# Layer B's value product: the low pass with 72 weight columns, issued between transposes, two half steps behind a head's last transposes

## The chip, the cores and the metric

One core of one Trainium2 chip runs the kernel. The metric is the device time of one execution in microseconds (us); smaller is better. Runs of one kernel differ by about 0.2%.

## What is computed

Two attention layers of a streaming encoder, over a prompt of 2048 tokens and a sample of 64 tokens, with model width 1024. Each layer normalises x, makes queries, keys, values and a gate by one input projection, attends, multiplies by the gate, projects out and adds x. The change touches layer B (the second one): 16 heads of 64 dimensions, each 64-token chunk attends to itself and the 8 chunks before it. For one chunk of one head, cut to what matters:

```python
s = einsum('bqkgd,bskd->bkgqs', q, k) * 64**-0.5 + bias   # scores
p = softmax(where(valid, s, NEG_INF))
o = einsum('bkgqs,bskd->bqkgd', p, v)                      # value product
y = x + (o * silu(gate)) @ w_out
```

## The kernel before

All matrix products are done on TensorE (PE) with 32-bit numbers split in two parts, a high part that the fast format holds and a low part, the rest. A product of two such numbers is then high x high, high x low and low x high.

**Units and heads.** Layer B works on `its`, 72 items: 8 pairs of heads, each over 9 units (eight units of 256 prompt tokens, as two tiles of 128, and the sample of 64 tokens, which comes ahead of the last prompt unit). Within an item the loop of `pipeline` (L1199) runs over four steps `y`: tile 0 and tile 1 of the first head, then of the second; the sample has two steps.

**What a step does.** `scores` (L1080) multiplies queries by keys into a bank `sb` of PSUM; DVE adds the bias and takes the row minimum (L1114), ACT takes the exponential (L1118). Then comes filler: the projections of later units, cut in small pieces (`filler.to`, lines L481 to L483), paced by `goal`. Then `values` (L1135) for the step before: one transpose of p on PE per 128 keys (up to five, all recorded at the helper's line L597), and `split_to`: ACT writes the high part `ph` (L569), DVE the low part `pl` (L570). `ph` and `pl` have two buffers each, one per head.

**The value product.** `outputs` (L1163) takes one head of one unit, all its tiles together. V lies in `VT` with 128 columns per 128 keys: 64 of its high part, 64 of its low part. For each block of keys it issues two products with the same 128 weight columns, one that streams `ph` (L1188) and one that streams `pl` (L1189), so all four combinations are summed. A full unit has four blocks that stream 256 columns and two that stream 128. The first head's product opens the bank `o` (one buffer). With the second head, `outputs` first transposes the gate `G` into the bank `tp` (L1171 to L1173; ACT reads it in `gate_t`, L973), and after the product `finish_pairs` runs: two copies on ACT (L981), two additions on DVE (L983), one product on POOL (L984), one store on SP's queue (L985).

**Where the product stands.** A head whose last transposes were issued in one step has its product in the step after (`nxt`, `pend`): the first head's at y = 3, the second head's at y = 1 of the next unit.

**The bank tp.** It has one buffer, and `queries` (L1042) uses it too, at the end of step y = QY = 1 (for the sample y = 0), for the next unit: four transposes, then four ACT operations on the bank (L1062, L1063), and `low`, as background work, for each of two heads: two DVE operations that read the bank (L1067, L1071) and one that doesn't (L1075).

**What sets the order.** On PE the order of the program is kept (`manual_schedule`); on the other engines a planner orders the instructions by data and by a simulated timeline. Background work (`bg`) waits in a list; `bg.share` issues some of it after each `scores` and `values`, and it is tied behind the step's last work on that engine.

Of the kernel before, what the change touches and what calls it, by code (L numbers as in the profile page):

```python
# [15 lines left out]
P = 128  # L16
# [10 lines left out]
HD = 64  # L27
# [12 lines left out]
AL, AP_ = 0.7, 4  # L40
BL, BP_ = 1.8, 4
FR = 0.6
KEEP = [1, 1] + [0] * (NU - 1)

PACE_B = 2.45
# [6 lines left out]
def hybrid_encoder_kernel(  # L52
# [32 lines left out]
    nc = tc.nc  # L85
# [14 lines left out]
    def psum(tag, cols, bufs, pool=None):  # L100
        uid[0] += 1
        return (pool or pp).tile([P, cols], F32, tag=tag, name=f"{tag}_{uid[0]}", bufs=bufs)
# [174 lines left out]
    bg = Background()  # L277
# [317 lines left out]
    def transpose(out, in_):  # L595
        n = in_.shape[0]
        nc.tensor.transpose(out, in_, ident[:n, :n])  # L597
# [390 lines left out]
    def layer_b():  # L988
# [53 lines left out]
        def queries(it):  # L1042
            for q in it.todo:
                bg.run(q)
            u, T, tiles = it.unit
            gk = ksc[:, 1:2]
            if u == 1:
                load_cache(ckt_b[it.hp], cv_b[it.hp], CB, True)
            tp = psum("tp", 512, 1)
            for pr, (tt, t0, n) in zip(it.prs, tiles):  # L1050
                for j in range(2):
                    transpose(tp[:, j * T + t0 : j * T + t0 + n], pr[:n, j * P : (j + 1) * P])
            it.q1 = q1 = t("q1", [P, 2, UT], 2, F32R)
            it.q2 = q2 = low_queries().rearrange("p (h s) -> p h s", h=2)
            if u == NU:
                kd = [a[:, CB : CB + TS] for a in (KSA, KSB)]
            else:
                kd = [a[:, u * UT : (u + 1) * UT] for a in (KA, KB)]
            qt = [tp[r, 0:T] for r in halves]
            kt = [tp[r, T : 2 * T] for r in halves]  # L1060
            for hh, rows in enumerate(halves):
                nc.scalar.activation(q1[rows, hh, :T], qt[hh], AF.Identity, scale=qsc[rows, 1:2])  # L1062
                nc.scalar.activation(kd[hh][rows], kt[hh], AF.Identity, scale=gk[rows])  # L1063

            def low(hh, rows):
                def fn():
                    nc.vector.scalar_tensor_tensor(  # L1067
                        q2[rows, hh, :T], qt[hh], qsc[rows, 1:2], q1[rows, hh, :T].bitcast(F32),
                        op0=ALU.mult, op1=ALU.subtract,
                    )  # L1070
                    nc.vector.scalar_tensor_tensor(  # L1071
                        kd[hh][halves[1 - hh]], kt[hh], gk[rows], kd[hh][rows].bitcast(F32),
                        op0=ALU.mult, op1=ALU.subtract,
                    )
                    nc.vector.tensor_copy(q1[halves[1 - hh], hh, :T], q1[rows, hh, :T].bitcast(F32))  # L1075
                return fn

            it.todo = [bg.put(1.0, low(hh, rows), True) for hh, rows in enumerate(halves)]

        def scores(it, i, h):  # L1080
            u, T, tiles = it.unit
# [50 lines left out]
                        op=ALU.mult,  # L1132
                    )

        def values(it, i, h):  # L1135
            u, T, tiles = it.unit
            last = u == NU
            tt, t0, n = tiles[i]
            if i == 0:
                it.ph[h] = t("ph", [P, 6, 256], 2, F32R)  # L1140
                it.pl[h] = t("pl", [P, 6, 256], 2, F32R)
            if last:
                sizes, kb = [P, P, TS], 0
            else:
                kt0 = max(tt - 4, 0)
                sizes, kb = [P] * (tt - kt0 + 1), kt0 - it.base
            PT = psum_b("sb", 1024, 2)
            PTv = PT.rearrange("p (c x) -> p c x", x=P)
            for c, kn in enumerate(sizes):
                transpose(PTv[:kn, c, :n], it.p[i, h][:n, c * P : c * P + kn])  # L1150
            full = sum(kn == P for kn in sizes)
            groups = [(0, full, P)]
            if last:
                groups.append((2, 1, TS))
            for c, m, kn in groups:
                bg.anchor(*split_to(
                    it.ph[h][:kn, kb + c : kb + c + m, t0 : t0 + n],
                    it.pl[h][:kn, kb + c : kb + c + m, t0 : t0 + n],
                    PTv[:kn, c : c + m, :n],
                ))  # L1160
            it.sizes = sizes

        def outputs(it, h):  # L1163
            u, T, tiles = it.unit
            last = u == NU
            n = tiles[0][2]
            sizes = it.sizes
            if h == 0:
                it.O = psum("o", 512, 1)
            else:  # L1170
                GT = psum("tp", 512, 1)  # L1171
                for e, (_, t0, _) in enumerate(tiles):
                    transpose(GT[:, t0 : t0 + n], it.G[:n, e * P : (e + 1) * P])  # L1173
                gt = gate_t(GT[:, :T].rearrange("p (j s) -> p j s", j=1), T)
            mm = []
            if last:
                for c, kn in enumerate(sizes):
                    mm.append((VS[:kn, c, h], c, kn, 0, TS))
            else:
                ta, tb = tiles[0][0], tiles[1][0]  # L1180
                for kt in range(max(tb - 4, 0), ta + 1):
                    mm.append((VT[:, kt, h], kt - it.base, P, 0, UT))
                if ta >= 4:
                    mm.append((VT[:, ta - 4, h], ta - 4 - it.base, P, 0, P))
                mm.append((VT[:, tb, h], tb - it.base, P, P, UT))
            for x, (vt, c, kn, q0, q1_) in enumerate(mm):
                dst = it.O[:, h * T + q0 : h * T + q1_]
                nc.tensor.matmul(dst, vt, it.ph[h][:kn, c, q0:q1_], start=x == 0, stop=False)  # L1188
                nc.tensor.matmul(dst, vt, it.pl[h][:kn, c, q0:q1_], start=False, stop=x == len(mm) - 1)  # L1189
            if h == 1:  # L1190
                finish_pairs(
                    it.O[:, : 2 * T].rearrange("p (j e s) -> p j e s", j=1, e=2),
                    gt,
                    T,
                    og[1][:, it.hp : it.hp + 1, u * UT : u * UT + T],
                )
                finished[1, u] = finished.get((1, u), 0) + 1

        def pipeline():  # L1199
            filler.attending = False  # L1200
            bg.lazy = True
            for q in Q2:
                zero(q[0:64, 256:512])
            filler.to(its[1].mark - 5.12)
            queries(its[0])
            filler.to(its[1].mark)
            filler.attending = True
            prev = pend = None
            for x, it in enumerate(its):
                heads = [(i, h) for h in range(2) for i in range(len(it.unit[2]))]  # L1210
                c0 = filler.done
                end, near = c0 + (PACE_B if len(heads) == 4 else PACE_S) * len(heads), 1e9
                if x + 2 < len(its):
                    near = its[x + 2].mark
                    if len(its[x + 1].unit[2]) + len(its[x + 2].unit[2]) < 4:
                        near += MORE
                    end = max(its[x + 2].mark, min(end, its[x + 3].mark - 1.0 if x + 3 < len(its) else end))

                def goal(s):
                    filler.to(c0 + min((end - c0) * s / (2 * len(heads)), (near - c0) * s / NS))  # L1220

                for y, (i, h) in enumerate(heads):
                    scores(it, i, h)
                    bg.share(BL, BP_)
                    goal(2 * y + 1)
                    nxt = None
                    if prev is not None:
                        values(*prev)
                        bg.share(BL, BP_)
                        if prev[1] == len(prev[0].unit[2]) - 1:  # L1230
                            nxt = prev[0], prev[2]
                    prev = it, i, h
                    if pend is not None:
                        outputs(*pend)
                    pend = nxt
                    goal(2 * y + 2)
                    if y == (QY if len(heads) == 4 else QS) and x + 1 < len(its):
                        queries(its[x + 1])
                        near = 1e9
                assert x + 2 >= len(its) or its[x + 2].ready  # L1240
            values(*prev)
            filler.to(filler.done + 2.6)
            if pend is not None:
                outputs(*pend)
            filler.to(filler.done + 2.6)
            outputs(prev[0], prev[2])

        return pipeline

# [175 lines left out]
```

## Time and profile before

| | |
|---|---|
| time, median of 3 runs | 2327.18 us (2323.96 to 2329.47) |
| profiled execution, span | 2323.8 us |
| what lies around the span | 3.4 us, median less span |
| instructions | 42433 |
| TensorE granted clock, mean | 0.998 |
| layer B's attention | from about 905 to 2166 us (first and last L1188) |

The profile is one execution on the chip. PE is a matmul, PEld the load of its weights; a load runs beside the matmul before it. The time of a matmul in a row is a modelled one and overlaps the next one's; what it costs in a stream is read from the distance between starts. In a group's row stand the line, the engine, the operation, what it writes and reads, the shape and the count, then busy time, the mean of one in ns, and after the second bar the idle time of the engine before it and what ended that. In a timeline's row stand start, duration (us), engine and line; idle time stands in brackets. In a row by windows the last three figures are the granted clock of TensorE, the DMA engines' share and GB/s.

### The profile page before, as it was taken

The page shows a single profiled execution, that of the slowest core. Times are in us where ns is not written, and L with a number is a line of the kernel's source. Part 1 is how long each engine was busy: PE and PEld are TensorE (multiplying, and loading weights), DVE is VectorE, ACT ScalarE, POOL GpSimd, SP SyncE. Part 2 cuts the span into 40 slices and gives each one's busy share as a digit, 9 for nine tenths or more (in the row PEclk, how much of TensorE's full clock was granted, in tenths as well). Part 3 has the DMA queues.
Part 4 walks back from the last instruction along what each step waited for, and adds up shares of the span by engine and source line. Part 5 has one row for each costly group of instructions (what it writes and reads, how often), then busy time and mean ns, then how long its engine had stood idle before and what let it go on. Part 6 is the DMA issues. An engine that isn't in the chain of part 4 may idle for free.

```text
span 2323.8 us, 42433 instructions
## 1 busy us (share of the span) xinstructions
PE 2269.6 (98%) x13981; PEld 1985.2 (85%) x13981; DVE 1547.3 (67%) x5214; ACT 1432.7 (62%) x3644; POOL 847.6 (36%) x1194
## 2 busy tenths in 40 slices
PE   8899999999999998999999999999999999999999
PEld 7787888888889997878888888888888888888999
DVE  7679988887782228876766767767667677676211
ACT  7778777777772236765665656656656566566321
POOL 5554533333254446432222222222222222224443
PEclk9999999999999999999999999999999999999999
DMA  8846446754446776453444533534435435433664
GB/s 256 263 146 207 162 144 195 229 167 162 134 126 204 226 216 219 145 186 126 158 142 128 161 127 114 178 126 152 143 123 163 134 103 177 131 126 106 189 186 148
DMA packets 232126, 379.37 MB, mean 163 GB/s; under 512 B 24721, under 2 KB 163361, under 8 KB 231873
## 3 DMA queue, kind: packets, MB, share of 16 engines
q1 hardware_dynamic: 231904, 376.65, 51.3%
q8 instruction: 110, 1.80, 0.3%
q14 instruction: 112, 0.91, 0.1%
HBM read 296.13 MB, written 82.08 MB: 163 GB/s over the span
## 4 chain that ended last, share of the span: by engine, by line
PE 77%; DVE 10%; ACT 5%; DMA 5%; issue 2%; POOL 1%; SPq 0%; POOLq 0%; ACTq 0%; DVEq 0%
PE pj L481 13%; PE pj L483 12%; PE pj L482 12%; PE pj L1283 5%; PE pj L1284 5%; PE pj L1285 5%; PE sb L597 5%; PE o L1189 3%; PE o L1188 3%; PE tp L597 3%; PE sb L1110 3%; PE sb L1111 3%; PE sa L597 2%; DVE sq L524 1%; DVE p L1114 1%
## 5 line engine op out<-in xcount | busy, mean ns | idle before, releaser
L481 PE MATMUL pj<-wh,xx 128*128 128x512 f32 (+1 forms) x1648 | 668.7, 406 | 15.2 <-DVE ms L433 7.2
L483 PE MATMUL pj<-wh,xx 128*128 128x512 f32 (+1 forms) x1648 | 638.1, 387 | 0.0
L482 PE MATMUL pj<-wl,xx 128*128 128x512 f32 (+1 forms) x1648 | 635.0, 385 | 0.0
L483 PEld LDWEIGHTS pj<-wh,xx 128*128 128x128 f32 x1648 | 310.4, 188 | 67.3
L481 PEld LDWEIGHTS pj<-wh,xx 128*128 128x128 f32 x1648 | 311.9, 189 | 56.9 <-ACT pb L504 6.5
L386 POOL TENSOR_TENSOR xx<-xraw,xx 128x528 fp32r<-128x528 f32 (+1 forms) x200 | 265.6, 1344 | 218.2 <-ACT xx L385 212.0
L482 PEld LDWEIGHTS pj<-wl,xx 128*128 128x128 f32 x1648 | 312.5, 190 | 37.7
L528 POOL TENSOR_TENSOR f<-f,mhalf 128x4 f32<-128x4 f32 (+3 forms) x221 | 227.9, 1031 | 228.7 <-DVE f L524 216.9
L1118 ACT ACTIVATE p<-p,nm 128x640 f32<-128x640 f32 (+5 forms) x272 | 204.4, 751 | 167.2 <-DVE nm L1114 165.1
L1283 PE MATMUL pj<-xx,wh 128*128 128x264 f32 x1024 | 293.3, 286 | 0.1
L1284 PE MATMUL pj<-xx,wh 128*128 128x264 f32 x1024 | 291.3, 284 | 0.0
L1285 PE MATMUL pj<-xx,wl 128*128 128x264 f32 x1024 | 289.8, 283 | 0.0
L1114 DVE CUSTOM_DVE_ANT_0 p<-sb,BT 128x640 f32<-128x640 f32 (+5 forms) x272 | 196.7, 723 | 119.6 <-PE sb L1111 116.2
L570 DVE TENSOR_TENSOR pl<-sb,ph 128x640 fp32r<-128x640 f32 (+5 forms) x288 | 196.8, 683 | 116.1 <-ACT ph L569 113.7
L385 ACT CAST xx<-xraw 128x528 fp32r<-128x528 f32 (+1 forms) x200 | 123.4, 626 | 220.3 <-PE pj L1285 131.9
L984 POOL TENSOR_TENSOR o<-gt,o 128x256 f32<-128x256 f32 (+2 forms) x140 | 107.4, 767 | 371.3 <-issue 149.0
L569 ACT CAST ph<-sb 128x640 fp32r<-128x640 f32 (+5 forms) x288 | 167.1, 580 | 122.4 <-PE sb L597 114.0
L1288 DVE TENSOR_TENSOR res<-pj,res 128x264 f32<-128x264 f32 x128 | 55.1, 431 | 246.5 <-PE pj L1285 230.7
L1283 PEld LDWEIGHTS pj<-xx,wh 128*128 128x128 f32 x1024 | 192.7, 188 | 0.8 <-DVE res L1288 0.3
L1285 PEld LDWEIGHTS pj<-xx,wl 128*128 128x128 f32 x1024 | 192.6, 188 | 0.0
L1284 PEld LDWEIGHTS pj<-xx,wh 128*128 128x128 f32 x1024 | 192.4, 188 | 0.2
L524 DVE CUSTOM_DVE_ANT_0 sq<-pa 128x64 f32<-128x64 f32 (+1 forms) x850 | 170.2, 253 | 22.1 <-ACT pa L504 20.0
(189 smaller groups left out, 4810.5 us busy)
## 6 DMA issues: line engine op xcount, KB each, us to landing
xx<-xsb SPq DMA_DIRECT2D x224, 512.0 KB, 4.1
xx<-xsa SPq DMA_DIRECT2D x88, 512.0 KB, 4.8
xraw<-oga SPq DMA_DIRECT2D x64, 264.0 KB, 3.4
xraw<-ogb SPq DMA_DIRECT2D x64, 264.0 KB, 3.3
xsa<-xx SPq DMA_DIRECT2D x32, 512.0 KB, 4.0
wraw<-in_w_in_b_dram SPq DMA_DIRECT2D x64, 256.0 KB, 3.4
xsb<-xx SPq DMA_DIRECT2D x32, 512.0 KB, 3.8
xraw<-in_x_dram SPq DMA_DIRECT2D x40, 256.0 KB, 4.1
```

The costliest lines, as they stand in the source:

```text
L386: nc.gpsimd.tensor_tensor(xl, rv, xh.bitcast(F32), op=ALU.subtract)
L481: nc.tensor.matmul(ps[:n, :C], xh, wh, start=k == 0, stop=False)
L482: nc.tensor.matmul(ps[:n, :C], xh, wl, start=False, stop=False)
L483: nc.tensor.matmul(ps[:n, :C], xl, wh, start=False, stop=k == KC - 1)
L528: nc.gpsimd.tensor_tensor(fv, fv, mhalf[:n, :H], op=ALU.pow)
L570: b = nc.vector.tensor_tensor(dst_lo, src, dst_hi.bitcast(F32), op=ALU.subtract)
L597: nc.tensor.transpose(out, in_, ident[:n, :n])
L1114: mi = nc.vector.tensor_tensor_reduce(out=p[:n, :nk], in0=S[:n, o : o + nk], in1=bias[:n, b0 : b0 + nk], op0=ALU.add, op1=ALU.min, scale=1 ...
L1118: ex = nc.scalar.activation(p[:n, :nk], p[:n, :nk], AF.Exp, scale=-1.0, bias=nmh, accum_out=it.sm[:n, 2 * i + h : 2 * i + h + 1],)
L1283: nc.tensor.matmul(ps[:, :OT], wh, oh, start=k == 0, stop=False)
L1284: nc.tensor.matmul(ps[:, :OT], wh, ol, start=False, stop=False)
L1285: nc.tensor.matmul(ps[:, :OT], wl, oh, start=False, stop=k == KC - 1)
```

## The change

- `VM = HD + 8 = 72`. The pass that streams `pl` loads 72 weight columns instead of 128 (blocks of 64 keys keep 128), and writes 72 rows of `o`. So `pl` is multiplied by the high part of V and by 8 of the 64 columns of its low part; the other 56 columns of low x low are left out.
- `outputs` becomes a generator. It issues G's transposes (second head), then the first high product, then hands out the low products as a list, and issues the remaining high products at the end. The accumulation starts and stops with high products.
- `values` takes that list and issues one low product after each of its transposes, the rest at its end.
- In `pipeline`, `pend` is a list. A head's product is issued with the transposes of the second step after its last ones: the first head's at y = 0 of the next unit, together with the second tile of the second head, and the second head's at y = 2 of the next unit, together with the second tile of that unit's first head. `whole` issues a product in one piece, where two are pending before a new buffer of `ph` is taken (around the sample), and at the end.
- Ahead of G's transposes all of `low` that `queries` has left is issued.

```diff
+VM = HD + 8
...
-            it.todo = [bg.put(1.0, low(hh, rows), True) for hh, rows in enumerate(halves)]
+            st.low = it.todo = [bg.put(1.0, low(hh, rows), True) for hh, rows in enumerate(halves)]
...
-        def values(it, i, h):
+        def values(it, i, h, lows=()):
+            lows = list(lows)
...
                 transpose(PTv[:kn, c, :n], it.p[i, h][:n, c * P : c * P + kn])
+                if lows:
+                    lows.pop(0)()
...
             it.sizes = sizes
+            for low in lows:
+                low()
...
             else:
+                for q in st.low:
+                    bg.run(q)
                 GT = psum("tp", 512, 1)
...
-            for x, (vt, c, kn, q0, q1_) in enumerate(mm):
-                dst = it.O[:, h * T + q0 : h * T + q1_]
-                nc.tensor.matmul(dst, vt, it.ph[h][:kn, c, q0:q1_], start=x == 0, stop=False)
-                nc.tensor.matmul(dst, vt, it.pl[h][:kn, c, q0:q1_], start=False, stop=x == len(mm) - 1)
+            def high(x):
+                vt, c, kn, q0, q1_ = mm[x]
+                nc.tensor.matmul(
+                    it.O[:, h * T + q0 : h * T + q1_], vt, it.ph[h][:kn, c, q0:q1_],
+                    start=x == 0, stop=x == len(mm) - 1,
+                )
+
+            def low(x):
+                vt, c, kn, q0, q1_ = mm[x]
+                M = VM if kn == P else P
+                nc.tensor.matmul(
+                    it.O[:M, h * T + q0 : h * T + q1_], vt[:, :M], it.pl[h][:kn, c, q0:q1_],
+                    start=False, stop=False,
+                )
+
+            high(0)
+            yield [lambda x=x: low(x) for x in range(len(mm))]
+            for x in range(1, len(mm)):
+                high(x)
...
+            def whole(it, h):
+                out = outputs(it, h)
+                for low in next(out):
+                    low()
+                for _ in out:
+                    pass
+
+            prev, pend, step = None, [], 0
...
                     if prev is not None:
-                        values(*prev)
+                        step += 1
+                        if prev[1] == 0:
+                            while len(pend) > 1:
+                                whole(*pend.pop(0)[:2])
+                        out = lows = ()
+                        if pend and pend[0][2] < step - 1:
+                            out = outputs(*pend.pop(0)[:2])
+                            lows = next(out)
+                        values(*prev, lows)
+                        for _ in out:
+                            pass
                         bg.share(BL, BP_)
                         if prev[1] == len(prev[0].unit[2]) - 1:
-                            nxt = prev[0], prev[2]
+                            pend.append((prev[0], prev[2], step))
                     prev = it, i, h
-                    if pend is not None:
-                        outputs(*pend)
-                    pend = nxt
...
             values(*prev)
-            filler.to(filler.done + 2.6)
-            if pend is not None:
-                outputs(*pend)
-            filler.to(filler.done + 2.6)
-            outputs(prev[0], prev[2])
+            while pend:
+                whole(*pend.pop(0)[:2])
+            filler.to(filler.done + 5.2)
+            whole(prev[0], prev[2])
```

More of the change, by code (lines that the diff above doesn't have):

```diff
@@ L1207, in pipeline @@
             filler.attending = True
-            prev = pend = None
+            def whole(it, h):
[5 more added lines that the diff above has]
+            prev, pend, step = None, [], 0
             for x, it in enumerate(its):
@@ L1225, in pipeline @@
                     goal(2 * y + 1)
-                    nxt = None
                     if prev is not None:
-                        values(*prev)
+                        step += 1
[9 more added lines that the diff above has]
+                            pass
                         bg.share(BL, BP_)
                         if prev[1] == len(prev[0].unit[2]) - 1:
-                            nxt = prev[0], prev[2]
+                            pend.append((prev[0], prev[2], step))
                     prev = it, i, h
-                    if pend is not None:
-                        outputs(*pend)
-                    pend = nxt
                     goal(2 * y + 2)
```

## The prediction

> **What bounds the kernel now.** I read the page first: the span, the busy times, the chain that ended last.
>
> ```profile
> span 2323.8 us, 42433 instructions
> ...
> PE 2269.6 (98%) x13981; PEld 1985.2 (85%) x13981; DVE 1547.3 (67%) x5214; ACT 1432.7 (62%) x3644; POOL 847.6 (36%) x1194
> ...
> PE 77%; DVE 10%; ACT 5%; DMA 5%; issue 2%; POOL 1%; SPq 0%; POOLq 0%; ACTq 0%; DVEq 0%
> ```
>
> TensorE (PE) is busy for 98% of the span and makes 77% of the chain, with DVE at 67% and ACT at 62%. It takes its instructions in the order of the program, so whatever shortens or stops its stream moves the end by as much. The profiled span of 2323.8 us lies 3.4 us under the median of the runs, 2327.18 us; I sum against the span and add 3.4 at the end. What a run of this kernel can tell from no change is about 0.2%, some 5 us.
>
> Next, the groups of instructions with shapes kept apart, for the operations that the change touches.
>
> ```profile
> L1189 PE MATMUL o<-pl,VT 128*128 128x256 f32 x448 | 114.2, 286 | 2.5 <-DVE pl L570 2.5
> L597 PE MATMUL tp<-ident,G 128*128 128x128 f32 x256 | 49.5, 275 | 1.9 <-DVE KB L1071 1.9
> ```
>
> The durations (286, 275 ns) overlap one another, so they are no prices; a price is the distance between starts. The low products waited 2.5 us for pl in all. The second row matters most: a transpose of G has waited for L1071 on DVE, the last reader of the tp bank.
>
> **The product's own time on PE.** The timeline of PE at the end of one head's product:
>
> ```profile
> 1501.66 0.28 PE L1189 MATMUL o<-pl,VT 128*128 128x256 f32 x1
> 1501.78 0.22 PE L1188 MATMUL o<-ph,VT 128*128 128x128 f32 x1
> 1501.84 0.27 PE L1189 MATMUL o<-pl,VT 128*128 128x128 f32 x1
> 1501.95 0.28 PE L1188 MATMUL o<-ph,VT 128*128 128x128 f32 x1
> 1502.06 0.27 PE L1189 MATMUL o<-pl,VT 128*128 128x128 f32 x1
> ```
>
> A product over 256 moving columns follows the last after 0.12 us. One over 128 should take half, and the first step is 0.06, but then the steps are 0.11: there the load of 128 weight columns is the limit. What a shorter load does behind transposes, the weight loads show:
>
> ```profile
> 1505.17 0.36 PEld L597 LDWEIGHTS tp<-ident,pa 128*128 128x128 f32 x3
> 1505.50 0.14 PEld L1110 LDWEIGHTS sb<-KSB,q 128*64 128x64 f32 x1
> 1505.61 0.14 PEld L1111 LDWEIGHTS sb<-KSB,q 128*64 128x64 f32 x1
> 1505.67 0.14 PEld L1110 LDWEIGHTS sb<-KSB,q 128*64 128x64 f32 x1
> ```
>
> Loads of 64 columns step by 0.06 us (1505.61 to 1505.67), but the first one behind a transpose steps by 0.11 (1505.50 to 1505.61), as the transposes do (three loads in 0.33). A load can start only when the matmul before has begun, and that one waited for the transpose. So a transpose holds the array for 0.11 us itself; it isn't its load that is long. Then a low product put between two transposes costs the same 0.11 + 0.12 as before, and its shorter load hides nothing new.
>
> What is left is the product over 128 columns that follows another low product: 0.06 instead of 0.11 with 72 columns. A full head has 6 low products for the 5 transposes of one step, so one such place each, in 8 pairs of heads x 6 units x 2 heads = 96 heads: 96 x 0.05 = 4.8 us. The 16 sample heads have three short low products, at most 16 x 3 x 0.05 = 2.4 us. I take 6 us off, and 2.5 us for the wait on pl, which goes since pl is a half step older. Bound: if a transpose did leave the array after 0.06, 5 low products a head would gain 0.05 each, 24 us more. The number of products, high ones and transposes stays as it is.
>
> **What moves with it.** The first head's product moves to the next unit's step 0, the second's to its step 2. With each goes all it issues: two ACT copies (L981), two DVE adds (L983), the POOL product (L984), and the store on SP's queue (L985), which nobody reads before the last projection; these cost nothing as long as the o bank's next product is a half step off. Transposes with products between take 5 x 0.23 = 1.15 us instead of 0.55, so ph and pl come 0.6 us later. They are used two half steps later, and a half step of scores and filler lies before the next transposes into that bank: I cost it at nothing. Without that cover it would be 0.6 us a step.
>
> Not hidden is the transpose of G. It moves with the second head's product from ahead of the next queries to behind them. There is one tp bank, and queries' transposes fill it at the end of step 1. G's transposes, now at the head of step 2's values, must wait until the four ACT and four DVE operations on that bank are over. That DVE has to finish is no guess; at the very end of layer B the old order meets the same:
>
> ```profile
> 2136.15 0.41 PE L597 MATMUL tp<-ident,G 128*128 128x128 f32 x2 [1.43 <-DVE KB L1071]
> ```
>
> G's two transposes began after 1.43 us of idle PE, which that bank's last reader on DVE ended. Behind them on PE wait the product, step 2's transposes, the filler projections and the next scores. To price it I take, unit by unit, the place where the change puts G (the first transpose of p after the queries) and the end of the last L1071. Four such places, two rows or three each:
>
> ```profile
> 1303.74 0.71 PE L597 MATMUL sb<-ident,p 128*128 128x128 f32 x5
> ...
> 1305.50 0.49 DVE L1071 SCALAR_TENSOR_TENSOR KB<-tp,ksc,KB 64x256 fp32r<-64x256 f32 x1
> ```
>
> ```profile
> 1440.55 0.71 PE L597 MATMUL sb<-ident,p 128*128 128x128 f32 x5
> ...
> 1442.10 0.56 DVE L533 TENSOR_TENSOR pa<-pa,f 128x256 f32<-128x256 f32 x1
> 1442.61 0.82 DVE L570 TENSOR_TENSOR pl<-sb,ph 128x640 fp32r<-128x640 f32 x1
> 1443.47 0.49 DVE L1067 SCALAR_TENSOR_TENSOR q<-tp,qsc,q 64x256 fp32r<-64x256 f32 x1
> 1443.97 0.49 DVE L1071 SCALAR_TENSOR_TENSOR KB<-tp,ksc,KB 64x256 fp32r<-64x256 f32 x1
> ```
>
> ```profile
> 920.07 0.60 PE L597 MATMUL sb<-ident,p 128*128 128x128 f32 x4
> ...
> 925.39 0.68 DVE L570 TENSOR_TENSOR pl<-sb,ph 128x512 fp32r<-128x512 f32 x1
> ...
> 926.60 0.49 DVE L1071 SCALAR_TENSOR_TENSOR KB<-tp,ksc,KB 64x256 fp32r<-64x256 f32 x1
> ```
>
> ```profile
> 2120.42 0.71 PE L597 MATMUL sb<-ident,p 128*128 128x128 f32 x5
> ...
> 2121.83 0.29 DVE L1071 SCALAR_TENSOR_TENSOR KSB<-tp,ksc,KSB 64x64 fp32r<-64x64 f32 x1
> ```
>
> First place: 1305.99 - 1303.74 = 2.25 us. Second: 1444.46 - 1440.55 = 3.91, less L570's 0.82, which depends on those transposes and so will come after; 3.09. Third, in the first pair of heads, where DVE also squares activations: 927.09 - 920.07 - 0.68 = 6.34. Fourth, where the queries are the sample's: 1.70. The wait arises in every unit that issues queries at step 1 and has a unit before it: 8 x 9 less 8 sample units, the first and the last, 62. By kind I count 19 like the first, 30 like the second, 8 like the fourth, 5 like the third: 42.8 + 92.7 + 13.6 + 31.7 = 181 us. If DVE also puts L533 (0.56) behind the bank's readers, the second kind is 2.53 and the sum 164; the quoted members are long ones of their kinds, so I take 164. The floor is a DVE that is always free: in the first place ACT's last conversion ends at 1303.63
>
> ```profile
> 1303.17 0.46 ACT L1063 ACTIVATE KB<-tp,ksc 64x256 fp32r<-64x256 f32 x1
> ```
>
> and two DVE operations of 0.49 follow, 1304.61, a wait of 0.87: 62 x 0.87 = 54 us.
>
> A wait of this length may also lower the clock. The profile's windows around one long wait, and one of 2.00 us:
>
> ```profile
> 1005.20:1008.60 3.40, 1.16 (x9) 0.95 (x7) 3.25 (x8) 0.88 (x3) 0.35 (x1) 1.00 1.00 321
> 1008.60:1015.40 6.80, 5.51 (x22) 5.02 (x23) 3.77 (x16) 3.50 (x8) 2.94 (x6) 0.50 0.37 124
> 865.20:868.60 3.40, 3.10 (x14) 2.56 (x15) 2.64 (x4) 0.93 (x2) 2.36 (x2) 1.00 0.84 300
> ```
>
> ```profile
> 1009.89 0.80 PE L481 MATMUL pj<-wh,xx 128*128 128x512 f32 x1 [3.53 <-DVE ms L433]
> ```
>
> ```profile
> 865.50 0.47 PE L481 MATMUL pj<-wh,xx 128*128 128x512 f32 x1 [2.00 <-ACT xx L385]
> ```
>
> The granted clock (the last figure but two) went to 0.50 at 1008.6, 2.2 us into a wait of 3.53 us, and PE lost half of 1009.89 to 1015.40, 2.75 us. After 2.00 us of waiting it stayed at 1.00. The 49 waits of 2.25 and 3.09 us lie between; I let half of them trip it at half that price, 24.5 x 1.4 = 34 us, and the 5 long ones at the full 2.75, 14 us: 48. Ends: 14 and 49 x 1.7 + 14 = 97. [...]
>
> Sum: 2323.8 - 6 - 2.5 + 164 + 48 = 2527, with 3.4 for a run 2531 us.
>
> **The rivals.** (1) The other side: DVE gets through the tp bank before G comes, so nothing waits and only the saving is left: 2323.8 - 8.5 + 3.4 = 2319 us, with the 24 us bound 2295. For it speaks one unit in nine, where queries are issued a half step earlier. Against it: in 62 places the bank's last reader ends 1.3 to 7 us after the place where G now comes. It decides at a wait of about 0.14 us a place, 8.5/62. (2) The wait shrinks to its floor, no clock trip: 2323.8 - 8.5 + 54 + 3.4 = 2373. (3) Waits as forecast, but every one trips the clock in full: 62 x 2.75 = 171 instead of 48, 2654. (4) A load of 72 columns is slower than one of 128. The steps of 0.06 against 0.11 for 64 columns speak against it. If the 0.14 us that such a load's record shows (1505.50) stood open at each of the 720 low products (16 heads x (2 + 4 + 6 x 6 + 3)), 101 us came on top, 2632. [...] (5) The change does less than it says: with a transpose that is not limited by its load, interleaving saves nothing; that is in the forecast.
>
> **How the numbers follow.** Forecast 0.81, (1) 0.08, (2) 0.06, (3) and (4) together 0.05. The forecast's own ends are 2324 - 33 + 130 + 14 = 2435 and 2324 - 6 + 181 + 97 = 2596; towards (2) and (3) I widen to 2400 to 2610. Only (1) ends faster or the same: faster by over 0.2% 0.07, within 0.2% 0.03 (a few waits left against the saving), slower 0.90.
>
> **What would show it.** Right: G's transposes into tp carry waits of 1 to 6 us ended by DVE L1071, about 62 of them, the idle time before that group growing from 1.9 to over 100 us; PE's share of busy time falls to about 92%; stretches of layer B at a clock under 1.00; low products start 0.11 us after a transpose and the transpose 0.12 after them. Wrong: G's group without waits, or L1067 and L1071 done ahead of step 2's first transposes; then the time stays near 2319. If low products between transposes step by clearly less than 0.23 a pair, my price of a transpose is wrong.

## The result and the profile after

The changed kernel takes 2530.89 us (2528.86 to 2533.23) where the kernel before, run beside it, takes 2327.34 us: a ratio of 1.0878, 95% interval 1.0863 to 1.0893, 8.8% slower. The forecast was 2531 us, range 2400 to 2610.

The page of the changed kernel: span, busy times, the chain that ended last, and two of its groups (line, engine, operation, shape and count, busy time, mean in ns, then the idle time of PE before the group and what ended it). Its lines lie one to a few dozen further down than before.

```profile
span 2531.5 us, 42462 instructions
...
PE 2338.9 (92%) x13981; PEld 2042.8 (81%) x13981; DVE 1548.3 (61%) x5214; ACT 1447.5 (57%) x3644; POOL 847.6 (33%) x1194
...
PE 78%; DVE 12%; ACT 4%; DMA 4%; issue 2%; POOL 0%; SPq 0%; ACTq 0%; DVEq 0%; POOLq 0%
...
L598 PE MATMUL sb<-ident,p 128*128 128x128 f32 (+2 forms) x1168 | 239.7, 287 | 2.4 <-DVE pl L571 1.6
...
L598 PE MATMUL tp<-ident,G 128*128 128x128 f32 (+1 forms) x272 | 57.1, 291 | 153.3 <-DVE KB L1072 141.9
```

The last row is the answer: PE stood idle for 153.3 us ahead of G's transposes, where it was 1.9 us, and DVE's reads of the tp bank (L1072, which was L1071 in the kernel before) ended most of it. DVE's work hardly grew (1548 us against 1547), yet its share of the chain did. Before p's transposes the idle time is 2.4 us; the kernel before had 8.1 there (the second experiment, which leaves them alone, shows the same 8.1).

PE's busy time went up by 69 us as well, though its 13981 instructions are as many as before and some are shorter. Layer B by itself, as one window in each kernel, separates the added idle time from the added busy time (length, then PE busy, PEld, DVE, ACT, POOL; the last figures are the granted clock, the DMA share and GB/s). Before:

```profile
905.00:2166.00 1261.00, 1242.97 (x7373) 1071.58 (x7373) 883.90 (x2947) 796.05 (x1996) 378.35 (x566) 1.00 0.44 142
```

After:

```profile
905.00:2373.00 1468.00, 1310.22 (x7369) 1125.62 (x7368) 885.96 (x2953) 811.63 (x2000) 379.09 (x566) 0.95 0.40 122
```

The stretch is 207 us longer, the whole difference of the spans. PE's idle time in it rose from 18 to 158 us (+140), its busy time by 67 us at a mean clock of 0.95.

One place in the timeline of the changed kernel, and the windows behind it:

```profile
1323.75 0.49 DVE L1072 SCALAR_TENSOR_TENSOR KB<-tp,ksc,KB 64x256 fp32r<-64x256 f32 x1
...
1324.38 0.66 PE L598 MATMUL tp<-ident,G 128*128 128x128 f32 x2 [2.83 <-DVE KB L1072]
```

```profile
1324.00:1327.30 3.30, 2.92 (x15) 2.95 (x16) 0.66 (x2) 0.58 (x2) 0.00 (x0) 0.50 0.00 0
1327.30:1330.70 3.40, 3.40 (x18) 2.92 (x18) 2.65 (x6) 1.58 (x5) 0.74 (x1) 1.00 0.00 0
```

DVE leaves the bank at 1324.24, G follows at 1324.38 after 2.83 us of idle PE, and the window from 1324.00 to 1327.30 runs at half clock, through the whole interleaved product. There are 62 waits of over 1 us before G. Read in this way from the timeline and the clock of the trace, they give a table:

| wait before G | places | of these, followed by a stretch at half clock |
|---|---|---|
| 1.2 to 1.6 us | 7 | 0 |
| 2.0 to 2.3 us | 18 | 5 |
| 2.5 to 2.6 us | 14 | 11 |
| 2.7 to 3.0 us | 20 | 18 |
| 3.3 to 4.7 us | 3 | 3 |

### The profile page after: what moved, and what is told of

Read it like the earlier page. It is cut to its first block, busy times and chain, and to the rows that moved or that the text cites. A ratio compares the mean times of both kernels' runs of the same rounds, so it can differ in the third digit from the quotient of the medians.

```text
span 2531.5 us, 42462 instructions
## 1 busy us (share of the span) xinstructions
PE 2338.9 (92%) x13981; PEld 2042.8 (81%) x13981; DVE 1548.3 (61%) x5214; ACT 1447.5 (57%) x3644; POOL 847.6 (33%) x1194
## 4 chain that ended last, share of the span: by engine, by line
PE 78%; DVE 12%; ACT 4%; DMA 4%; issue 2%; POOL 0%; SPq 0%; ACTq 0%; DVEq 0%; POOLq 0%
PE pj L482 12%; PE pj L484 12%; PE pj L483 12%; PE sb L598 6%; PE pj L1318 5%; PE pj L1319 5%; PE pj L1320 5%; PE o L1196 4%; PE o L1204 3%; PE tp L598 3%; PE sb L1111 3%; PE sb L1112 3%; DVE q L1068 2%; DVE p L1115 2%; PE sa L598 2%
## 5 line engine op out<-in xcount | busy, mean ns | idle before, releaser
L482 PE MATMUL pj<-wh,xx 128*128 128x512 f32 (+1 forms) x1648 | 684.6, 415 | 11.7 <-ACT pb L505 5.3
L484 PE MATMUL pj<-wh,xx 128*128 128x512 f32 (+1 forms) x1648 | 647.8, 393 | 0.0
L483 PE MATMUL pj<-wl,xx 128*128 128x512 f32 (+1 forms) x1648 | 646.1, 392 | 0.0
L484 PEld LDWEIGHTS pj<-wh,xx 128*128 128x128 f32 x1648 | 317.5, 193 | 70.2
L482 PEld LDWEIGHTS pj<-wh,xx 128*128 128x128 f32 x1648 | 321.0, 195 | 58.1 <-ACT pb L505 6.9
L483 PEld LDWEIGHTS pj<-wl,xx 128*128 128x128 f32 x1648 | 321.2, 195 | 39.5 <-DVE wl L316 0.4
L598 PE MATMUL sb<-ident,p 128*128 128x128 f32 (+2 forms) x1168 | 239.7, 287 | 2.4 <-DVE pl L571 1.6
L598 PE MATMUL tp<-ident,G 128*128 128x128 f32 (+1 forms) x272 | 57.1, 291 | 153.3 <-DVE KB L1072 141.9
L1318 PEld LDWEIGHTS pj<-xx,wh 128*128 128x128 f32 x1024 | 192.7, 188 | 0.7
```

Of the source, the lines that this page charges most:

```text
L482: nc.tensor.matmul(ps[:n, :C], xh, wh, start=k == 0, stop=False)
L483: nc.tensor.matmul(ps[:n, :C], xh, wl, start=False, stop=False)
L484: nc.tensor.matmul(ps[:n, :C], xl, wh, start=False, stop=k == KC - 1)
L1318: nc.tensor.matmul(ps[:, :OT], wh, oh, start=k == 0, stop=False)
```

## The experiments

The theory: G's transposes, moved behind the next queries' transposes, wait for the one tp bank, and the waits lower the clock. The main rival: the interleaving, which draws the transposes apart and makes ph and pl later, costs the time. All run beside the kernel before, 2325.79 us in the first four, 2327.95 us in the last three.

**1. G's transposes back ahead of the queries, all else as changed.**

```diff
+        def turn_gate(it):
...
+            for q in st.low:
+                bg.run(q)
+            GT = psum("tp", 512, 1)
...
-            else:
-                for q in st.low:
-                    bg.run(q)
-                GT = psum("tp", 512, 1)
...
+            elif it.gt is None:
+                turn_gate(it)
...
                         for _ in out:
                             pass
+                        for q, qh, at in pend:
+                            if qh == 1 and at == step - 1:
+                                turn_gate(q)
```

> The changed kernel, with G's transposes and ACT's read of them back at their old place (step 1, ahead of the next queries); product, 72 columns and interleaving as changed. Theory (the wait for the tp bank and the lowered clock that follows it): the waits before G's transposes fall from 153 us to about 2, the clock stays at 1.00 in layer B, and what is left is the saving of some 8 us: 2319 us. Rival (interleaving itself, or the later ph and pl, costs the time): stays at about 2530 us.

Measured: 2324.18 us, 0.9990 of before (0.9981 to 0.9999). The groups of the transposes into tp:

```profile
L598 PE MATMUL tp<-ident,pa 128*128 128x128 f32 x384 | 63.8, 275 | 12.0 <-ACT gt L974 8.8 <-ACT wh L313 2.0 <-DVE pa L534 1.2
L598 PE MATMUL tp<-ident,G 128*128 128x128 f32 x256 | 49.5, 275 | 1.9 <-DVE KB L1073 1.9
```

The wait is gone (1.9 us, as before), and with it the slowing; interleaving and the late product stay, so they were not the cause. The same bank now makes a smaller wait in the other direction. The product used to stand between G's transposes and the queries'; without it the queries' transposes wait 8.8 us in all for ACT to read G's result, where the kernel before had 1.2 us. The median lies 5 us above the forecast of 2319 us. Whether this wait is the reason is not shown: the profiled execution has the wait too, and at 2318.47 us, the fastest of eleven, it is on the forecast.

**2. 72 columns alone.** The kernel before, with `vt[:, :VM]` and `it.O[:VM, ...]` in the pass that streams pl, and the last pair issued low first.

> The kernel before, with 72 weight columns in the low pass and nothing else (the last pair is issued low first, so that the accumulation stops with a high product). Theory (a load limits only products over 128 or 64 columns, by 0.05 us): two such places in each of 96 full heads, 9.6 us, and one to three in the others, 2 to 3 us more: 2315 us, more than the interleaved order saves, which has one such place a head. Rival (loads were hidden or 72 columns load no faster): 2327 us. Rival (72 columns load slower than 128): above 2340 us.

Measured: 2315.11 us, 0.9949 (0.9936 to 0.9961): as expected. The end of one head's product in PE's timeline (start, us):

```profile
1885.06 0.22 PE L1190 MATMUL o<-ph,VT 128*128 128x128 f32 x1
1885.12 0.29 PE L1190 MATMUL o<-pl,VT 128*72 128x128 f32 x2
1885.25 0.27 PE L1190 MATMUL o<-ph,VT 128*128 128x128 f32 x1
1885.36 0.45 PE L482 MATMUL pj<-wh,xx 128*128 128x512 f32 x1
```

High, low, low take 0.19 us to the last high product (1885.06 to 1885.25), a step of 0.06 each; before, the same three steps took 0.06 and twice 0.11. And p's transposes wait as they did before:

```profile
L598 PE MATMUL sb<-ident,p 128*128 128x128 f32 x1120 | 165.3, 274 | 8.1 <-DVE nm L1115 5.5 <-DVE pl L571 1.4 <-ACT sq L542 0.7
```

So the 72 columns alone are worth 11 us, without any of the change's reordering.

**3. No interleaving, product as late as in the change.** `lows = next(out)` and the list given to `values` make place for `whole(*pend.pop(0)[:2])` ahead of `values(*prev)`.

> The changed kernel without interleaving: at the same steps the whole product, G's transposes first, is issued in one piece ahead of the step's transposes. Theory (tp bank): the same waits, 2525 to 2540 us. Rival (interleaving): the time goes back to 2315 to 2330 us.

Measured: 2539.45 us (one run). G's group with shapes kept apart, in the changed kernel and here:

```profile
L598 PE MATMUL tp<-ident,G 128*128 128x128 f32 x256 | 53.4, 292 | 134.1 <-DVE KB L1072 122.8 <-DVE KSB L1072 11.4
```

```profile
L598 PE MATMUL tp<-ident,G 128*128 128x128 f32 x256 | 54.1, 296 | 135.7 <-DVE KB L1072 121.1 <-DVE KSB L1072 11.4 <-POOL VT L550 3.3
```

The waits are those of the changed kernel (135.7 us against 134.1) without any interleaving, so the loss does not need it.

**4. All of step 2's filler ahead of G.**

```diff
-                    goal(2 * y + 1)
+                    goal(2 * y + (2 if y == 2 else 1))
```

> The changed kernel, with all of step 2's filler ahead of G's transposes instead of half of it: each of the 62 waits should shrink by the moved filler, about 1.2 us. Theory with the clock: 153 us of waits become about 80, all of them under 2 us, so the clock isn't lowered any more, and the 60 us that it cost go too: about 2395 us. Theory without the clock (waits alone): 2455 us. Rival (interleaving): 2530 us.

Measured: 2386.85 us, 1.0249 of before (1.0225 to 1.0273). G's group, and layer B as one window:

```profile
L598 PE MATMUL tp<-ident,G 128*128 128x128 f32 x256 | 50.8, 280 | 62.1 <-DVE KB L1072 56.9 <-POOL VT L550 4.2 <-DVE KSB L1072 1.0
```

```profile
905.00:2228.00 1323.00, 1246.15 (x7383) 1068.52 (x7382) 885.85 (x2962) 812.96 (x2011) 376.92 (x569) 1.00 0.45 136
```

The time fell by 144 us. Of that, idle time in layer B is 81 us (158 to 77), most of it ahead of G (134.1 to 62.1 in this form). All but two of the waits before G are now under 2 us. The rest is the clock: its mean is 1.00 again, and PE is busy for 1246 us with the instructions that took 1310 in the changed kernel. The clock's part of the loss is about these 64 us.

**5. Interleaved with 128 columns.** The first experiment's kernel with `VM = P`.

> The first experiment's kernel (G's transposes ahead of the queries, products interleaved, two half steps late) with 128 weight columns in the low pass. Theory (a transpose and a load of 128 columns both take 0.11 us, so interleaving hides nothing by itself): a full head with its five transposes takes the 2.18 us that it took before, not the 2.12 us of 72 columns, and the time is that of before within 5 us, 2325 to 2331 us. Rival (interleaving hides weight loads): 2.12 us a head or less and 2315 to 2320 us.

Measured: 2330.82 us, 1.0011 (1.0002 to 1.0020). A full head with its five transposes, from the first instruction to the second filler projection behind it, in the kernel before, in the changed one, and here:

```profile
1500.27 0.71 PE L597 MATMUL sb<-ident,p 128*128 128x128 f32 x5
...
1502.45 0.39 PE L482 MATMUL pj<-wl,xx 128*128 128x512 f32 x1
```

```profile
1742.15 0.28 PE L1196 MATMUL o<-ph,VT 128*128 128x256 f32 x1
...
1744.28 0.39 PE L483 MATMUL pj<-wl,xx 128*128 128x512 f32 x1
```

```profile
1902.59 0.28 PE L1201 MATMUL o<-ph,VT 128*128 128x256 f32 x1
...
1904.78 0.39 PE L483 MATMUL pj<-wl,xx 128*128 128x512 f32 x1
```

They take 2.18, 2.13 and 2.19 us: interleaving hides nothing by itself. The 0.05 us a head that the change saves come from the 72 columns.

**6. Queries one step later.** `QY = 2` in the changed kernel, so that they come behind G.

> The changed kernel with the next unit's queries one step later (QY = 2), so that they come behind G's transposes instead of ahead of them. Theory (tp bank): the waits of G's transposes end and the clock stays up, 2320 us; where the later queries delay the next unit's first scores, at most 64 new waits of 0 to 1 us, up to 2370 us. Rival (interleaving or the late product): 2530 us.

Measured: 2346.00 us, 1.0070 (1.0055 to 1.0086). G no longer waits, but the next unit's scores do (groups with shapes taken together):

```profile
L598 PE MATMUL tp<-ident,G 128*128 128x128 f32 (+1 forms) x272 | 52.8, 273 | 0.0
L1111 PE MATMUL sb<-KA,q 128*128 128x384 f32 (+2 forms) x240 | 73.6, 310 | 11.4 <-DVE q L1076 7.9 <-DVE KA L1072 2.4 <-ACT p L1119 0.8
L1112 PE MATMUL sb<-KA,q 128*128 128x384 f32 (+2 forms) x240 | 71.2, 313 | 6.9 <-DVE q L1068 6.7
```

These are 18 us of new waits, nearly all for the results of DVE's `low`, whose reads of the bank G waited for in the changed kernel. The clock of layer B has a mean of 0.99. The time falls by 185 us when the two users of the bank change places. It stays above the 2320 us that were expected without new waits; how the difference divides between waits and clock was not taken apart.

**7. Another order of a head's products.** The second experiment's kernel, in which wide products (256 columns) and narrow ones (128) are mixed: h for high, l for low, 4 and 5 narrow.

Not the code, but the order that it issues:

```diff
-  h0 l0 h1 l1 h2 l2 h3 l3 h4 l4 l5 h5
+  h0 h1 h2 h4 l0 h5 l1 l2 l4 l5 l3 h3
```

> The second experiment's kernel (before, with 72 columns alone) with the twelve products of a head in another order: each product over 128 columns is followed by one of 72 weight columns, and each load of 128 columns lies behind a product over 256. Theory (load or stream, whichever is longer): the four narrow products of a full head take 0.06 us each instead of two of them 0.11, another 0.094 us x 96 heads = 9 us, and in the 16 heads of the second unit 0.05 each, 1 us: 2305 us. Rival (narrow products have a floor of their own near 0.11 us, or pl comes too late): 2315 us.

Measured: 2304.08 us (2302.18 to 2306.69), 0.9896 of before (0.9883 to 0.9910), the fastest of all. A full head with its transposes:

```profile
1645.12 0.71 PE L598 MATMUL sb<-ident,p 128*128 128x128 f32 x5
...
1646.09 0.28 PE L1190 MATMUL o<-pl,VT 128*72 128x256 f32 x1
1646.21 0.22 PE L1190 MATMUL o<-ph,VT 128*128 128x128 f32 x1
1646.27 0.65 PE L1190 MATMUL o<-pl,VT 128*72 128x256 f32 x5
1646.76 0.28 PE L1190 MATMUL o<-ph,VT 128*128 128x256 f32 x1
1646.88 0.39 PE L482 MATMUL pj<-wh,xx 128*128 128x512 f32 x1
1647.11 0.40 PE L483 MATMUL pj<-wl,xx 128*128 128x512 f32 x1
```

h5 takes 0.06 us (1646.21 to 1646.27), and l1 l2 l4 l5 l3 together 0.49, which is three wide steps of 0.12 and two narrow ones of 0.06. The narrow products cost their own 0.06, and the head with its transposes takes 1.99 us (1645.12 to 1647.11) where it took 2.18 before.

## Why the prediction was right

**The wait (step "Not hidden is the transpose of G").** Right in place, cause and count: 62 waits, ended by DVE's last read of the tp bank. The sum was 164 us. Measured are 153.3 us of idle time in all, 151 more than before, and a little that the idle time hides: it counts from the modelled end of the projection ahead, 0.39 us after its start, where the stream would have gone on after 0.23:

```profile
1328.11 0.39 PE L482 MATMUL pj<-wh,xx 128*128 128x512 f32 x1
1328.33 0.39 PE L483 MATMUL pj<-wl,xx 128*128 128x512 f32 x1
1328.56 0.39 PE L484 MATMUL pj<-wh,xx 128*128 128x512 f32 x1
```

0.16 us at 62 places are 10 us, 161 in all. Its kinds: the commonest short wait was read as 2.25 us and is 2.24, the commonest long one as 3.09, or 2.53 with L533 behind, and is 2.83 (1324.38 above). That the sum is so near is in part luck. The five waits in the first pair of heads were priced at 31.7 us in all and came to 16.9, while the other 57, priced at 132, came to 136, or about 145 with what the idle time hides. The first place, priced at 6.34 us, waited 3.86 (the second row is one of the commonest short waits):

```profile
923.89 0.41 PE L598 MATMUL tp<-ident,G 128*128 128x128 f32 x2 [3.86 <-DVE KB L1072]
```

```profile
1368.90 0.41 PE L598 MATMUL tp<-ident,G 128*128 128x128 f32 x2 [2.24 <-DVE KB L1072]
```

At the first place DVE's operations stand in another order than before: its four reads of the bank follow one another (921.77 to 923.75), where squares, a row minimum and a `pl` stood between them (921.41 to 927.09). Experiments 1, 3, 4 and 6 show the cause from four sides: take away the wait with the interleaving kept, keep it with the interleaving gone, shorten it, turn it round.

**The clock.** Forecast 48 us; the trace gives 64 us of busy time (experiment 4 against the changed kernel). Half of the waits between 2.25 and 3.09 us were to trip it; of the 52 between 2.0 and 3.0 us 34 did, two in three, and with the three longer ones the clock fell 37 times, at 1.7 us each (64 us over 37). The forecast had it that such waits lower the clock, but the half was a guess: it went by the length of a wait, and the length alone does not decide (last section). The 1.7 us in the forecast's upper end stands beside no row, and no run shows it for all 49 waits: 34 of the 52 in the table cost it. The stretches at half clock last 3.4 us (27 of them) or twice that (10), and 35 of the 37 came behind waits shorter than 3.4 us.

**The saving.** Forecast 8.5 us. Waits and clock together make 161 + 64 = 225 us where the span grew by 208, so some 17 us were saved. The head's own part is as forecast (2.18 to 2.13 us, 5 us in 96 heads). Beside it went not only the 2.5 us for pl: p's transposes also waited 5.7 us less (8.1 to 2.4). The last 4 us are no more than what two other groups on PE waited less: the queries' transposes (5.7 to 3.4 us) and the first of each three filler projections (15.2 to 11.7). The claim that interleaving hides no load stands by experiment 5, the steps of 0.06 for 72 columns by experiments 2 and 7. Rival (4), a slower load of 72 columns, found no support. One sign came out otherwise: a low product was to start 0.11 us after a transpose and the next transpose 0.12 after that. The records show 0.02 and 0.20:

```profile
1742.27 0.27 PE L598 MATMUL sb<-ident,p 128*128 128x128 f32 x1
1742.29 0.36 PE L1204 MATMUL o<-pl,VT 128*72 128x256 f32 x1
1742.49 0.27 PE L598 MATMUL sb<-ident,p 128*128 128x128 f32 x1
```

The pair takes 0.22 us, so its price of 0.23 holds; how it divides between the two does not.

**The sum.** 2531 against 2530.89 is closer than its terms: the clock was 16 us too low, the saving 8 us too low and the wait 3 us too high, which nearly cancel. The 4 us that are left (a span of 2531.5 us where 2527 was forecast) are met by luck too: the median of the runs lies 0.6 us under the profiled span, not 3.4 above it. The mechanism is shown; the closeness of the number is not its merit. Rivals (1) to (3) fell: the bank was not free in time, the waits did not shrink to the floor of 54 us, and not every wait tripped the clock.

## What to carry to other kernels

When a step is moved, list every buffer with one copy that it takes, and read from the trace of before when that buffer's last reader ends at the new place; here, on an engine busy for 98% of its time, that wait was the price. In this kernel the waits cost their own length (153.3 us before G), and some 1.7 us more each time that the clock fell. That happened to 34 of 52 waits between 2 and 3 us and to none of the seven under 1.6 us, so waits that can't be removed are worth shortening. When a shorter weight load is the aim, find the products that are shorter than a load (here 0.06 us against 0.11) and put short loads behind those alone; here 72 columns gave 0.5%, and with another order of twelve instructions 1%.

## What the runs showed of the hardware that was not expected

**When the clock fell.** It fell for waits that were shorter than the stretch of 3.4 us at half clock that they brought, and the longer the wait, the more often. The trace shows what else decides. The 37 stretches at half clock in layer B of the changed kernel start on one grid: any two starts differ by a whole multiple of 3.4133 us, to within 0.01 us (read from the trace's record of the clock). Two waits of one length, 2.23 us before G at 1549.08 and 2.24 us before G at 1368.90, with windows cut along that grid:

```profile
1545.74:1549.15 3.41, 1.18 (x6) 0.66 (x5) 3.10 (x8) 2.78 (x7) 0.45 (x1) 1.00 0.83 196
1549.15:1552.57 3.42, 3.42 (x17) 3.42 (x18) 0.00 (x0) 1.08 (x2) 0.00 (x0) 0.50 0.38 137
```

```profile
1364.84:1368.25 3.41, 1.82 (x10) 1.22 (x8) 3.15 (x8) 3.35 (x9) 0.00 (x0) 1.00 0.90 238
1368.25:1371.66 3.41, 2.76 (x22) 2.60 (x23) 0.94 (x3) 1.67 (x5) 0.46 (x1) 1.00 0.53 166
1371.66:1375.07 3.41, 3.41 (x20) 2.80 (x20) 3.20 (x16) 1.45 (x4) 1.92 (x3) 1.00 0.53 149
```

The first wait lies whole within one stretch of the grid. PE is idle for 2.23 us of that stretch (3.41 less 1.18), and the next one runs at half clock. The second wait lies across a border, with 1.59 us of idle PE on one side and 0.65 on the other, and the clock stays at 1.00. Counted in this way over layer B of the changed kernel, each of the 37 falls follows a stretch with over 1.95 us of idle PE, and none of the 346 stretches at full clock that stayed so has over 1.90 us. The trace of experiment 3 divides in the same way (46 falls, at least 1.92 us; 334 stretches without one, at most 1.90 us). In the other seven traces no stretch of layer B with over 1.90 us kept its clock either, but 4 of the 11 falls follow less idle time, 1.41 to 1.71 us. So idle PE within one stretch of the grid tells nearly all of it, and not everything; and no run here moved one wait against the grid with all else kept.

**A transpose and its load.** The prediction said of a transpose that its load isn't what is long. Experiment 3 speaks for both being 0.11 us: five high products there stand ahead of transposes.

```profile
1234.07 0.75 PE L1196 MATMUL o<-ph,VT 128*128 128x256 f32 x5
1234.65 0.73 PE L598 MATMUL sb<-ident,p 128*128 128x128 f32 x5
```

0.58 us is three steps of 0.12 and two of 0.11, so the transpose came 0.11 us after the narrow last product. That is the step of such a product ahead of a load of 128 columns in the kernel before; ahead of one of 72 it is 0.06 (experiment 7). It changes no price above. That a load starts only when the matmul before it has begun has no exception in layer B of the kernel before: each of the 7370 loads there starts after the start of that matmul, by 1 ns at the least.
